# The last two of four token blocks: norm weights from a spread row, transposition behind the last product, additions of two or four tiles

## The chip, the core and the metric

The kernel runs on one core of a Trainium2 chip. A core has TensorE (PE, matrix products and transpositions; PEld is its loading of the stationary operand), VectorE (DVE), ScalarE (ACT), GpSimd (POOL) and SyncE (SP, which here only issues transfers), each with its own queue of instructions that it takes in order. They share an on-chip memory (SBUF) and the products' accumulators (PSUM). Sixteen transfer engines move data between the chip's DRAM and SBUF. The metric is device time in microseconds, the median of three runs.

## The reference

Two layers work on 512 tokens of width 1024, in float32. The change touches only the very end of the second layer, its feed-forward part:

```python
f = rmsnorm(h, ln_ffn_pre[layer])
f = (jax.nn.silu(f @ w_ffn_gate[layer]) * (f @ w_ffn_up[layer])) @ w_ffn_down[layer]
h = h + rmsnorm(f, ln_ffn_post[layer])

def rmsnorm(x, g):
    y = xf * lax.rsqrt(jnp.mean(xf * xf, axis=-1, keepdims=True) + RMS_EPS)
    return (y * g.astype(jnp.float32)).astype(x.dtype)
```

For every token the last product's row of 1024 numbers is scaled by one number of that token (r) and by the 1024 weights `ln_ffn_post`, and added to h, which is the result.

## The kernel before

**Layout.** h lies transposed: a tile of 128 partitions for 128 of the 1024 features, with the 512 tokens along the free axis, and eight such tiles (k = 0 to 7, `h[:, k, :]`). The weights of all norms lie in the tile `gains`, a column of 128 for each k; so `residual` (L841) can take a weight as a scalar per partition.

**The last product.** `feed_forward(1, ...)` works through the 22 blocks of the hidden width in groups (2 to 8, 8 to 14, 14 to 18, 18 to 22; blocks 0 and 1 come first). For each group it makes the hidden values (`sevens`, with the w_gate and w_up loads), and then their product with w_down. These products have the tokens as rows: four token blocks `tb` of 128, each with two halves `dh` of 512 features, `ys[tb][dh]`. Each product of float32 numbers is three products of parts (L193 to L195). The loads of all weights go through four buffers named `raw` of 512 KB each on SyncE's queue, where each waits until VectorE has read what stood in its buffer.

**The tail.** The product of the last group is made block by block in `tail` (L790). For each block and half, 12 products of 512 columns run on TensorE, VectorE adds them to `ys` (L808), ScalarE squares and sums (L811); VectorE adds the sums to v (L813), GpSimd raises v to the power -1/2 to r (L262), and ScalarE scales both halves by r (L832). The second half of the last block is made in two pieces of 256 columns in one PSUM tile, so that TensorE waits with the second for VectorE's addition of the first; there, scaling is shared by VectorE (L827) and ScalarE (L828).

**The end.** `give(tb, order)` (L1347) turns the scaled block by eight transpositions on TensorE (`turned`, L839, into PSUM tiles `yt` with the tag "tr", of which there are two), adds each 128x128 tile to h with its weight (`residual`, L844, one VectorE instruction per tile), and issues the transfer of each group of tiles to `out`. Block tb - 1 is given behind the product of block tb, the last one behind eight products of zeros (`idle`, L88) that occupy TensorE while r is made. The last block's four transfers alternate between SyncE's queue and ScalarE's.

The order within an engine comes from a scheduler that may move an instruction ahead of others written before it, where it depends on nothing among them; the places where that shows are given with the change.

```python
zero = zeros()
for tb in range(TB):
    end = tail(tb)
    if tb:
        give(tb - 1, (range(4), range(4, 8)))
idle(8, zero, end)
give(TB - 1, (range(4, 6), range(2), range(6, 8), range(2, 4)), (nc.sync, nc.scalar))
```

Of the kernel before, what the change touches and what calls it, by code (L numbers as in the profile page):

```python
# [15 lines left out]
P = 128  # L16
T = 512
D = 1024
# [22 lines left out]
def hybrid(ctx: ExitStack, tc: tile.TileContext, i: dict, out: bass.AP):  # L41
# [4 lines left out]
    tp = ctx.enter_context(tc.tile_pool(name="temps", bufs=4))  # L46
    wp = ctx.enter_context(tc.tile_pool(name="weights", bufs=4))
    sp = ctx.enter_context(tc.tile_pool(name="small", bufs=8))
    pp = ctx.enter_context(tc.tile_pool(name="psum", bufs=3, space=PSUM))

    n_of = {}
# [2 lines left out]
    def name(s):  # L54
        n_of[s] = n_of.get(s, 0) + 1
        return f"{s}_{n_of[s]}"
# [10 lines left out]
    def temp(s, shape=(P, T), tag="t", bufs=4, dt=F32):  # L67
        return tp.tile(list(shape), dt, tag=tag, name=name(s), bufs=bufs)

    def small(s, n=4, dt=F32):  # L70
        return sp.tile([P, n], dt, tag=f"s{n}", name=name(s))
# [702 lines left out]
        return mix_tail(0, mixed, ys)  # L774


    def tail_of(xs, load, ys, eps=None, last=False):

        ws = {}
        nk = len(xs)

        def urgent(tb):
            return tc.high_priority() if tb == TB - 1 and not last else ExitStack()

        ss, v, r = small("ss", 12), small("v"), small("r")

        def tail(tb, halfway=None):  # L790
            if not ws:
                for dh in range(2):
                    for kp in range(nk // 2):
                        ws[kp, dh] = load(kp, dh, dh == 1)
            c = slice(tb, tb + 1)
            final = last and tb == TB - 1
            two = small("two", 1) if final else None
            at = [(0, 0, 4), (1, 0, 2), (1, 2, 4)] if final else [(0, 0, 4), (1, 0, 4)]
            for n, (dh, m0, m1) in enumerate(at):
                if m0 == 0:  # L800
                    o = ps("lg" if dh else "mm", s="y")
                cols = slice(m0 * P, m1 * P)
                for k in range(nk):
                    w = [part[:, m0:m1, :] for part in ws[k // 2, dh][k % 2]]
                    end = token_products(o[:, cols], xs[k], w, tb, k == 0, k == nk - 1)
                y = ys[tb][dh][:, cols]
                with urgent(tb):
                    V.tensor_add(y, o[:, cols], y)  # L808
                    junk = temp("sq", (P, T), "sq", 3, BF16)
                    one = ss[:, 3 * tb + n : 3 * tb + n + 1]  # L810
                    A.activation(junk[:, cols], y, AF.Square, scale=1.0 / 32, accum_out=one)  # L811
                    if n == len(at) - 1:
                        V.scalar_tensor_tensor(out=v[:, c], in0=one, scalar=run, in1=eps[:, c] if eps is not None else rms_eps,  # L813
                                               op0=ALU.add, op1=ALU.add)
                    elif n:
                        V.tensor_add(two, run, one)
                        run = two
                    else:
                        run = one
                if halfway and n == 0:  # L820
                    halfway()
            with urgent(tb):
                rsqrt(r[:, c], v[:, c], 1)
            if final:
                for m in (0, 2):
                    cols = slice(m * P, (m + 2) * P)
                    V.tensor_scalar_mul(ys[tb][1][:, cols], ys[tb][1][:, cols], r[:, c])  # L827
                    A.activation(ys[tb][0][:, cols], ys[tb][0][:, cols], AF.Copy, scale=r[:, c])  # L828
                return end
            with urgent(tb):  # L830
                for y in ys[tb]:
                    A.activation(y, y, AF.Copy, scale=r[:, c])  # L832

        return tail, ys

    def turned(ys, k, tbs, out):

        for n, tb in enumerate(tbs):
            PE.transpose(out[:, n * P : (n + 1) * P], ys[tb][k // 4][:, k % 4 * P : (k % 4 + 1) * P], ident)  # L839

    def residual(o, k, cols, post):  # L841

# [217 lines left out]
    def feed_forward(layer, phase, xp, meanwhile=None):  # L1060
# [283 lines left out]
    with tc.tile_pool(name="ffn1", bufs=4) as xp:  # L1344
        tail, ys = feed_forward(1, phase, xp)

    def give(tb, order, queues=(nc.sync,)):  # L1347

        c = (tb * P, (tb + 1) * P)
        for n, some in enumerate(order):  # L1350
            tr = ps("tr", s="yt")
            for x, k in enumerate(some):
                turned(ys, k, (tb,), tr[:, x * P : (x + 1) * P])
            for x, k in enumerate(some):
                residual(tr[:, x * P : (x + 1) * P], k, c, G_FFN_POST + 1)
            k0, k1 = some[0], some[-1] + 1
            queues[n % len(queues)].dma_start(out[:, k0:k1, c[0] : c[1]], h[:, k0:k1, c[0] : c[1]])
# [69 lines left out]
```

## Time and profile before

| | |
|---|---|
| median of three runs | 1115.33 us (1115.09 to 1115.86) |
| the profiled execution | 1114.41 us |
| its span, from the first instruction to the last | 1112.7 us |
| TensorE, VectorE, ScalarE, GpSimd busy | 99%, 80%, 59%, 2% of the span |
| mean granted TensorE clock | 0.999 of full speed |
| read from DRAM, written | 104.71 MB, 2.10 MB |

The profile's page gives busy time, a chain of work that ended last and groups of instructions. Views of the trace behind it list instructions in order of time (start, duration, engine, line, operation, tiles, and in brackets the idle time of the engine just before it with what ended it; xN merges N instructions in a row), sum up busy time and transfers over stretches of time, and group instructions by line and shape. Durations of neighbours in one queue overlap a little: the next instruction starts before the last one's duration is over, so the distance of two starts is shorter than a duration.

### The profile page before, as it was taken

The numbers are of one execution on the slowest core, as the hardware profiler recorded it, in microseconds if no ns is written. First come the engines' busy times: TensorE is split into PE (matmuls) and PEld (weight loads), VectorE is DVE, ScalarE is ACT, GpSimd is POOL, SyncE is SP. The second block draws the span as 40 slices with busy tenths as digits, with TensorE's granted clock in tenths as the row PEclk, the third lists the DMA queues.
The fourth block names the chain that finished last, engine by engine and source line by source line (L and its number), as shares of the span: only waits on it lengthen the run. The fifth ranks groups of instructions, "written<-read, shape, count | busy, mean of one in ns | idle before, by whom it ended". The sixth has DMA issues, their size and how long they took to land.

```text
span 1112.7 us, 19537 instructions
## 1 busy us (share of the span) xinstructions
PE 1103.1 (99%) x7409; PEld 1000.2 (90%) x7409; DVE 891.2 (80%) x1721; ACT 660.5 (59%) x1388; POOL 25.4 (2%) x41
## 2 busy tenths in 40 slices
PE   9999999999999999999999999999999999999998
PEld 6998889999899899998988888889999899899996
DVE  7879558998698588797968889858998598588776
ACT  7775468665265254477647667768665266255453
POOL 0000000000000000001000000000000000000000
PEclk9999999999999999999999999999999999999999
DMA  7522231334134233244232654431125234233222
GB/s 268 159 79 74 88 104 58 114 95 153 57 115 136 58 111 114 77 153 151 78 95 71 159 125 130 129 95 57 58 95 161 67 109 132 65 112 116 77 76 76
DMA packets 63557, 118.12 MB, mean 106 GB/s; under 512 B 5164, under 2 KB 39992, under 8 KB 63464
## 3 DMA queue, kind: packets, MB, share of 16 engines
q1 hardware_dynamic: 62584, 116.05, 34.5%
q8 instruction: 58, 0.95, 0.4%
q0 software_dynamic: 192, 0.52, 0.2%
q10 hardware_dynamic: 688, 0.31, 0.1%
q14 instruction: 35, 0.29, 0.1%
HBM read 104.71 MB, written 2.10 MB: 96 GB/s over the span
## 4 chain that ended last, share of the span: by engine, by line
PE 89%; DVE 5%; ACT 3%; issue 1%; DMA 1%; POOL 0%; SPq 0%; POOLq 0%; DVEq 0%; ACTq 0%
PE y L193 9%; PE y L195 9%; PE y L194 9%; PE a L195 5%; PE a L193 5%; PE a L194 5%; PE e L193 3%; PE e L195 3%; PE x L193 3%; PE x L195 3%; PE e L194 3%; PE x L194 3%; PE ps L195 3%; PE ps L193 3%; PE ps L194 3%; PE v L193 2%
## 5 line engine op out<-in xcount | busy, mean ns | idle before, releaser
L241 ACT CAST whi<-raw 128x512 fp32r<-128x512 f32 x460 | 276.1, 620 | 261.3 <-PE y L195 118.6
L241 DVE TENSOR_TENSOR wlo<-raw,whi 128x512 fp32r<-128x512 f32 x460 | 305.8, 685 | 112.4 <-ACT whi L241 110.0
L193 PE MATMUL y<-whi,fhi 128*128 128x512 f32 (+1 forms) x356 | 139.8, 393 | 0.0
L194 PE MATMUL y<-wlo,fhi 128*128 128x512 f32 (+1 forms) x356 | 139.3, 391 | 0.0
L195 PE MATMUL y<-whi,flo 128*128 128x512 f32 (+1 forms) x356 | 139.3, 391 | 0.0
L193 PE MATMUL x<-xshi,whi 128*128 128x256 f32 x320 | 89.7, 280 | 0.0
L195 PE MATMUL x<-xshi,wlo 128*128 128x256 f32 x320 | 89.7, 280 | 0.0
L195 PE MATMUL a<-xshi,wlo 128*128 128x256 f32 x320 | 89.6, 281 | 0.0
L193 PE MATMUL a<-xshi,whi 128*128 128x256 f32 x320 | 89.6, 280 | 0.0
L194 PE MATMUL x<-xslo,whi 128*128 128x256 f32 x320 | 89.6, 280 | 0.0
L194 PE MATMUL a<-xslo,whi 128*128 128x256 f32 x320 | 89.5, 280 | 0.0
L195 PEld LDWEIGHTS y<-whi,flo 128*128 128x128 f32 x356 | 66.9, 188 | 15.6 <-DVE flo L241 0.2
L193 PEld LDWEIGHTS y<-whi,fhi 128*128 128x128 f32 x356 | 66.8, 188 | 15.0 <-DVE y L808 0.2
L194 PEld LDWEIGHTS y<-wlo,fhi 128*128 128x128 f32 x356 | 66.9, 188 | 14.9 <-DVE wlo L241 0.2
L195 PE MATMUL ps<-xshi,wlo 128*128 128x256 f32 (+1 forms) x224 | 66.7, 299 | 1.3 <-DVE wlo L241 1.3
L193 PE MATMUL ps<-xshi,whi 128*128 128x256 f32 (+1 forms) x224 | 67.7, 303 | 0.0
L194 PE MATMUL ps<-xslo,whi 128*128 128x256 f32 (+1 forms) x224 | 66.5, 297 | 0.0
L194 PEld LDWEIGHTS a<-xslo,whi 128*128 128x128 f32 x320 | 60.3, 188 | 0.3
L193 PEld LDWEIGHTS a<-xshi,whi 128*128 128x128 f32 x320 | 60.3, 188 | 0.3
L195 PEld LDWEIGHTS x<-xshi,wlo 128*128 128x128 f32 x320 | 60.3, 189 | 0.0
L193 PEld LDWEIGHTS x<-xshi,whi 128*128 128x128 f32 x320 | 60.3, 188 | 0.0
L194 PEld LDWEIGHTS x<-xslo,whi 128*128 128x128 f32 x320 | 60.3, 188 | 0.0
(291 smaller groups left out, 3086.7 us busy)
## 6 DMA issues: line engine op xcount, KB each, us to landing
raw<-in_w_gate SPq DMA_DIRECT2D x44, 512.0 KB
raw<-in_w_up SPq DMA_DIRECT2D x44, 512.0 KB
raw<-in_w_down SPq DMA_DIRECT2D x44, 512.0 KB
raw<-in_w_out SPq DMA_DIRECT2D x16, 512.0 KB
raw<-in_w_b_q SPq DMA_DIRECT2D x8, 512.0 KB
raw<-in_w_a_v SPq DMA_DIRECT2D x6, 512.0 KB
raw<-in_w_a_u SPq DMA_DIRECT2D x6, 512.0 KB
raw<-in_w_v SPq DMA_DIRECT2D x6, 512.0 KB
```

The source lines that it names most:

```text
L193: PE.matmul(o, w[0], x[0], start=start, stop=False, skip_group_check=more)
L194: PE.matmul(o, w[0], x[1], start=False, stop=False, skip_group_check=more)
L195: return PE.matmul(o, w[1], x[0], start=False, stop=stop, skip_group_check=more)
L241: last_parts[:] = A.copy(hi, src), (eng or V).tensor_sub(lo, src, hi)
```

## The change

The weights of the last norm are written, by a transfer of 1024 elements of 4 bytes, as a row into a DRAM tile (`row_of_gains`, at the start of the third group of layer 1), and later loaded from there into all 128 partitions of a `raw` buffer (`spread_gains`, behind the first tail). For blocks 2 and 3 (`added`) VectorE multiplies `ys` by that row into new tiles `yg`, ahead of r. ScalarE scales `yg`. The last block's second half is multiplied by r and the row in one VectorE instruction. The additions to h then need no weight and take two or four tiles at once (`give_added`). Block 2 is turned behind the last product (`end`), its last four tiles are added behind the last v (`sums`), there are six products of zeros instead of eight, and the PSUM tiles of the last block have the tags "lg" and "mm", of three buffers each.

```diff
+    def row_of_gains(block):
+        gain_row[0] = dp.tile([1, D], F32, name="row")
+        with tc.issue_after(last_load[0].ins), nc.allow_non_contiguous_dma(reason="one row of gains"):
+            nc.sync.dma_start(gain_row[0].rearrange("o (k p) -> (o k) p", k=KT),
+                              i["gains"][:, block * KT : block * KT + KT].rearrange("p k -> k p"))
+
+    def spread_gains():
+        row = gain_row[0]
+        gain_row[0] = wp.tile([P, D], F32, tag="raw", name=name("raw"), bufs=4)
+        nc.sync.dma_start(gain_row[0], row[0, :].partition_broadcast(P))
...
+            added = last and tb >= TB - 2
             final = last and tb == TB - 1
+            if added:
+                gained[tb] = [plain("yg") for _ in range(2)]
...
                     V.tensor_add(y, o[:, cols], y)
+                    if added and not (final and dh):
+                        V.tensor_mul(gained[tb][dh][:, cols], y, gain_row[0][:, 512 * dh + m0 * P : 512 * dh + m1 * P])
...
                     cols = slice(m * P, (m + 2) * P)
-                    V.tensor_scalar_mul(ys[tb][1][:, cols], ys[tb][1][:, cols], r[:, c])
-                    A.activation(ys[tb][0][:, cols], ys[tb][0][:, cols], AF.Copy, scale=r[:, c])
-                return end
+                    y0, y1 = (y[:, cols] for y in gained[tb])
+                    V.scalar_tensor_tensor(out=y1, in0=ys[tb][1][:, cols], scalar=r[:, c],
+                                           in1=gain_row[0][:, 512 + m * P : 512 + (m + 2) * P],
+                                           op0=ALU.mult, op1=ALU.mult)
+                    A.activation(y0, y0, AF.Copy, scale=r[:, c])
+                return end, total
             with urgent(tb):
-                for y in ys[tb]:
+                for y in gained[tb] if added else ys[tb]:
                     A.activation(y, y, AF.Copy, scale=r[:, c])
+            return end, total
...
+            if layer and gi == 2:
+                row_of_gains(G_FFN_POST + 1)
...
+    def give_added(tb, order, tags, queues=(nc.sync,), end=None, held={}):
+        c = (tb * P, (tb + 1) * P)
+        for n, some in enumerate(order):
+            tr = ps(tags[n], (P, len(some), P), s="yt")
+            k0, k1 = some[0], some[-1] + 1
+            with behind([end] if end else ()):
+                for x, k in enumerate(some):
+                    row_turned(gained[tb], k, tr[:, x, :])
+            with behind(held.get(n, ())):
+                V.tensor_add(h[:, k0:k1, c[0] : c[1]], tr, h[:, k0:k1, c[0] : c[1]])
+            queues[n % len(queues)].dma_start(out[:, k0:k1, c[0] : c[1]], h[:, k0:k1, c[0] : c[1]])
...
     for tb in range(TB):
-        end = tail(tb)
-        if tb:
+        end, sums = tail(tb)
+        if tb == 0:
+            spread_gains()
+        elif tb < TB - 1:
             give(tb - 1, (range(4), range(4, 8)))
-    idle(8, zero, end)
-    give(TB - 1, (range(4, 6), range(2), range(6, 8), range(2, 4)), (nc.sync, nc.scalar))
+    give_added(TB - 2, (range(2), range(2, 4), range(4, 8)), ("tr", "tr", "mm"), end=end, held={2: [sums]})
+    idle(6, zero, end)
+    give_added(TB - 1, (range(4, 6), range(2), range(6, 8), range(2, 4)), ("lg", "mm") * 2, (nc.sync, nc.scalar))
```

Three places in the order of the instructions. Line numbers after the change are higher by up to 46, and buffer numbers differ. First VectorE at the end of the program, before; y_9713 is the second half of the last block, yt_13423 and yt_13433 are block 2's turned tiles, the other yt the last block's:

```order
L816 TENSOR_TENSOR two_13368<-ss_13174 128x1
L844 SCALAR_TENSOR_TENSOR h<-yt_13423,gains,h 128x128 x2
L808 TENSOR_TENSOR y_9713<-y_13385,y_9713 128x256
L844 SCALAR_TENSOR_TENSOR h<-yt_13433,gains,h 128x128 x2
L813 SCALAR_TENSOR_TENSOR v_13175<-ss_13174,two_13368,eps_13170 128x1
L844 SCALAR_TENSOR_TENSOR h<-yt_13433,gains,h 128x128
L827 TENSOR_SCALAR y_9713<-y_9713,r_13176 128x256 x2
L844 SCALAR_TENSOR_TENSOR h<-yt_13433,gains,h 128x128
L844 SCALAR_TENSOR_TENSOR h<-yt_13452,gains,h 128x128 x2
L844 SCALAR_TENSOR_TENSOR h<-yt_13458,gains,h 128x128 x2
L844 SCALAR_TENSOR_TENSOR h<-yt_13464,gains,h 128x128 x2
L844 SCALAR_TENSOR_TENSOR h<-yt_13470,gains,h 128x128 x2
```

The same place after the change; raw_13260 is the spread row, yt_13436, yt_13441 and yt_13446 are block 2's:

```order
L837 TENSOR_TENSOR two_13380<-ss_13178 128x1
L827 TENSOR_TENSOR y_9715<-y_13398,y_9715 128x256
L1387 TENSOR_TENSOR h<-yt_13436,h 128x2x128
L1387 TENSOR_TENSOR h<-yt_13441,h 128x2x128
L834 SCALAR_TENSOR_TENSOR v_13179<-ss_13178,two_13380,eps_13174 128x1
L1387 TENSOR_TENSOR h<-yt_13446,h 128x4x128
L849 SCALAR_TENSOR_TENSOR yg_13379<-y_9715,r_13180,raw_13260 128x256 x2
L1387 TENSOR_TENSOR h<-yt_13465,h 128x2x128
L1387 TENSOR_TENSOR h<-yt_13460,h 128x2x128
L1387 TENSOR_TENSOR h<-yt_13470,h 128x2x128
L1387 TENSOR_TENSOR h<-yt_13475,h 128x2x128
```

All of block 2's additions now stand behind the last addition of y (L808 before, L827 after), two of them ahead of v and one between v and the scaling; none is left behind the scaling. Of the last block's tiles those that ScalarE scales (yt_13465) come first.

TensorE around the second half of the last product, before: four and one transpositions of block 2 stand between the two halves, three behind the last product.

```order
L195 MATMUL y_13385<-whi_13216,flo_12893 128x256
L839 MATMUL yt_13423<-ident,y_9710 128x128 x4
L839 MATMUL yt_13433<-ident,y_9711 128x128
L193 MATMUL y_13385<-whi_13202,fhi_12610 128x256
```

TensorE behind the last product, after: eight transpositions, then the products of zeros, of which the first is shown, then the last block's pairs in another order than they are written in.

```order
L196 MATMUL y_13398<-whi_13220,flo_12897 128x256
L867 MATMUL yt_13436<-ident,yg_13318 128x128 x2
L867 MATMUL yt_13441<-ident,yg_13318 128x128 x2
L867 MATMUL yt_13446<-ident,yg_13319 128x128 x4
L89 LDWEIGHTS zeros_13182
L89 MATMUL idle_13453<-zeros_13182 128x512
```

Nothing of block 2 is left between the halves. On SyncE's queue after the change, the row's transfer stands between the last w_down load of the second group and the w_gate loads of the third:

```order
L170 DMA raw_11828<-in_w_down 128x4x256
L170 DMA raw_11862<-in_w_down 128x4x256
L784 DMA row<-in_gains 1024x1x1
L147 DMA raw_11906<-in_w_gate 128x1024
L147 DMA raw_11908<-in_w_gate 128x1024
```

Before, the w_gate loads followed directly. The spreading load likewise comes right behind the last four w_down loads, ahead of all transfers to `out`.

More of the change, by code (lines that the diff above doesn't have):

```diff
@@ L48, in hybrid @@
     sp = ctx.enter_context(tc.tile_pool(name="small", bufs=8))
+    dp = ctx.enter_context(tc.tile_pool(name="rows", bufs=1, space=bass.MemoryType.DRAM))
     pp = ctx.enter_context(tc.tile_pool(name="psum", bufs=3, space=PSUM))
@@ L774, in layer_a @@
         return mix_tail(0, mixed, ys)
+    gained, gain_row = {}, [None]
+    def row_of_gains(block):
[7 more added lines that the diff above has]
+        nc.sync.dma_start(gain_row[0], row[0, :].partition_broadcast(P))
     def tail_of(xs, load, ys, eps=None, last=False):
@@ L812, in tail @@
                     if n == len(at) - 1:
-                        V.scalar_tensor_tensor(out=v[:, c], in0=one, scalar=run, in1=eps[:, c] if eps is not None else rms_eps,
+                        total = V.scalar_tensor_tensor(out=v[:, c], in0=one, scalar=run, in1=eps[:, c] if eps is not None else rms_eps,
                                                op0=ALU.add, op1=ALU.add)
@@ L838, in turned, with row_turned @@
         for n, tb in enumerate(tbs):
-            PE.transpose(out[:, n * P : (n + 1) * P], ys[tb][k // 4][:, k % 4 * P : (k % 4 + 1) * P], ident)
+            row_turned(ys[tb], k, out[:, n * P : (n + 1) * P])
+    def row_turned(y, k, out):
+        PE.transpose(out, y[k // 4][:, k % 4 * P : (k % 4 + 1) * P], ident)
     def residual(o, k, cols, post):
```

## The prediction

> **What bounds the kernel now.** I read the page first: matrix products fill the whole span, so a change elsewhere only counts where the products have stopped or are made to stop.
>
> ```profile
> PE 1103.1 (99%) x7409; PEld 1000.2 (90%) x7409; DVE 891.2 (80%) x1721; ACT 660.5 (59%) x1388; POOL 25.4 (2%) x41
> ```
>
> The change touches the last 20 us. The timeline of all engines from the last product on (start, duration, what ran) shows the stage that can move:
>
> ```profile
> 1103.76 0.28 PE L195 MATMUL y<-whi,flo 128*128 128x256 f32 x1
> ...
> 1103.88 0.49 PE L839 MATMUL yt<-ident,y 128*128 128x128 f32 x3
> 1104.08 0.42 DVE L808 TENSOR_TENSOR y<-y,y 128x256 f32<-128x256 f32 x1 [0.54 <-PE y L195]
> ...
> 1104.42 0.60 DVE L844 SCALAR_TENSOR_TENSOR h<-yt,gains,h 128x128 f32<-128x128 f32 x2
> ...
> 1104.86 0.19 ACT L811 ACTIVATION_READ_ACCUMULATOR sq<-y 128x1 f32 x1
> 1105.08 0.22 DVE L813 SCALAR_TENSOR_TENSOR v<-ss,two,eps 128x1 f32<-128x1 f32 x1
> ...
> 1105.38 0.55 POOL L262 TENSOR_TENSOR r<-v,mhalf 128x1 f32<-128x1 f32 x1 [6.29 <-DVE v L813]
> 1105.95 0.91 ACT L828 ACTIVATE y<-y,r 128x256 f32<-128x256 f32 x2 [0.91 <-POOL r L262]
> 1105.96 0.61 DVE L827 TENSOR_SCALAR y<-y,r 128x256 f32<-128x256 f32 x2 [0.40 <-POOL r L262]
> 1106.42 0.20 PEld L839 LDWEIGHTS yt<-ident,y 128*128 128x128 f32 x2 [0.83 <-PE idle L88]
> 1106.45 0.93 PE L839 MATMUL yt<-ident,y 128*128 128x128 f32 x4 [0.36 <-DVE y L827]
> 1106.49 2.75 DVE L844 SCALAR_TENSOR_TENSOR h<-yt,gains,h 128x128 f32<-128x128 f32 x9
> ```
>
> The last product ends at 1104.04. Add, square, sum, power and scaling follow one another to 1106.31 (1105.96 + 0.348, half of the x2 row). Then nine residual additions keep VectorE until 1109.24. The first of the nine is left over from block 2; the other eight are block 3's.
>
> After that only transfers run. Windows of the trace (stretch, busy time by engine, granted clock, DMA share, GB/s) show them:
>
> ```profile
> 1104.00:1104.50 0.50, 0.50 (x6) 0.37 (x5) 0.42 (x2) 0.00 (x0) 0.00 (x0) 1.00 0.02 7
> 1104.50:1105.00 0.50, 0.50 (x4) 0.21 (x3) 0.50 (x3) 0.47 (x2) 0.00 (x0) 1.00 0.99 283
> 1108.00:1109.00 1.00, 0.41 (x3) 0.20 (x2) 0.99 (x5) 0.00 (x0) 0.00 (x0) 1.00 1.00 286
> 1109.00:1110.00 1.00, 0.00 (x0) 0.00 (x0) 0.24 (x1) 0.00 (x0) 0.00 (x0) 1.00 0.99 282
> 1110.00:1110.50 0.50, 0.00 (x0) 0.00 (x0) 0.00 (x0) 0.00 (x0) 0.00 (x0) 1.00 0.76 220
> 1110.50:1111.00 0.50, 0.00 (x0) 0.00 (x0) 0.00 (x0) 0.00 (x0) 0.00 (x0) 1.00 0.32 92
> ```
>
> From 1108 to 1110 the transfer engines are full. Data moves until 1110.66 (0.32 of half a microsecond past 1110.5), and 2.0 us of completion follow to the span's end at 1112.7. The queues' table for 1103 to 1112.7 gives the price of a piece:
>
> ```profile
> q1 hardware_dynamic: 1600, 0.79, 28.4%
> q10 hardware_dynamic: 544, 0.26, 9.4%
> ```
>
> Together 37.8% of 9.7 us is 3.67 us for eight pieces of 128 KB: **0.46 us a piece**. From issue to first data I take **0.92 us**: an issue at 1103.57 answers to data at 1104.49 (0.02 of the window that ends at 1104.5).
>
> ```profile
> 1103.57 5.49 SPq L1357 DMA_DIRECT2D out<-h  x4
> ```
>
> **The change part by part.** *The multiplications by the row of weights.* Three 128x512 multiplications join VectorE before the last product, each as long as the 128x512 addition at 1096.76 below: 0.69, and 0.60 from its start to the next (a 128x128 residual takes 0.26 from start to start, by the x5 row). The idle time in front of the additions is their cover:
>
> ```profile
> 1096.76 0.69 DVE L808 TENSOR_TENSOR y<-y,y 128x512 f32<-128x512 f32 x1 [1.87 <-PE y L195]
> 1097.37 0.86 DVE L844 SCALAR_TENSOR_TENSOR h<-yt,gains,h 128x128 f32<-128x128 f32 x3
> ...
> 1098.38 1.38 DVE L844 SCALAR_TENSOR_TENSOR h<-yt,gains,h 128x128 f32<-128x128 f32 x5
> 1100.42 0.69 DVE L808 TENSOR_TENSOR y<-y,y 128x512 f32<-128x512 f32 x1 [0.66 <-PE y L195]
> 1101.86 0.42 DVE L808 TENSOR_TENSOR y<-y,y 128x256 f32<-128x256 f32 x1 [0.74 <-PE y L195]
> ```
>
> They fall one into each gap: 1.87, 0.66 and 0.74, leaving 1.27, 0.06 and 0.14. I cost them at 0. Without cover each would delay the second half of the last product by up to 0.60, since that half waits for the addition at 1101.86.
>
> *The five transpositions taken out from between the halves.* They save nothing: the second half begins when the addition of the first has ended (1101.86 + 0.42 = 1102.28), and it does so with them or without.
>
> ```profile
> 1102.34 0.19 PEld L193 LDWEIGHTS y<-whi,fhi 128*128 128x128 f32 x1 [0.21 <-DVE y L808]
> ```
>
> So the last product still ends at 1104.04. Behind it now stand eight transpositions instead of three (0.11 apart by the x3 row, done by 1104.95) and six idle products instead of eight, which wait for the first two-tile addition and end near 1106.4, before TensorE is wanted at 1106.59.
>
> *Block 2's additions.* ScalarE's operations keep their number and shapes. Before v there were two of 0.26; now there are two 128x256 ones, 0.34 from start to start (1104.08 to 1104.42). v, which ScalarE allows at 1105.05, goes from 1105.08 to 1105.10: **+0.02**. The four-tile addition starts 0.13 behind v and takes 0.60, so VectorE is free at 1105.83, before r at 1105.95. That addition replaces two residuals, one of which stood behind the scaling.
>
> *Block 3's scaling.* The multiplication by r and the row is a scalar_tensor_tensor; the groups by form show 478 ns for such an operation, against 348 now:
>
> ```profile
> L246 DVE SCALAR_TENSOR_TENSOR xslo<-h,gains,xshi 128x256 fp32r<-128x256 f32 x16 | 7.5, 478 | 0.1
> ```
>
> Its first half is ready at 1106.46, ScalarE's first half at 1105.97 + 0.51 = 1106.48, and TensorE now takes ScalarE's tiles first. With the 0.11 from data to weight load (1106.31 to 1106.42) the pair starts at 1106.59 and ends at 1107.03, against 1106.86 now: **+0.17**.
>
> *Block 3's additions.* Eight residuals, held up by two PSUM buffers, become four 128x256 additions of 0.42 (the row at 1104.08): 1107.07 + 3 x 0.34 + 0.42 = 1108.51, against 1109.24. **VectorE gains 0.73.** TensorE delivers all pairs by 1107.65 now that they have buffers of their own.
>
> *The transfers out.* Now block 2's last 256 KB is issued only at 1106.87 (behind the leftover residual, 1106.49 + 0.34), moves from 1107.79 to 1108.71, and pushes block 3's four pieces together; the last, issued at 1109.27 behind the last residual, ends at 1109.27 + 0.92 + 0.46 = 1110.65, which is what the windows show. In the changed kernel block 2's 256 KB leave at 1105.9 and are through at 1107.8. The pieces of block 3 are issued at 1107.5, 1107.85, 1108.2 and 1108.55. Data starts at 1108.44, and four pieces fill the engines for 1.84: **1110.28**. So of 0.73 only **0.38** reach the end; the limit moves from VectorE to the transfer engines. The bounds of this term are 0.73 (pieces don't wait for each other) and 0.
>
> *The row of weights.* Its 1024 elements go over SP's queue right behind the last w_down load of the group and ahead of two w_gate loads, whose landing VectorE does wait for:
>
> ```profile
> 940.63 0.37 SPq L169 DMA_DIRECT2D raw<-in_w_down  x1
> 942.98 0.34 SPq L146 DMA_DIRECT2D raw<-in_w_gate  x1
> ...
> 944.96 0.37 ACT L1015 COPY s<-a 128x256 f32<-128x256 f32 x1
> ...
> 950.03 0.69 DVE L988 TENSOR_TENSOR s<-raw,raw 128x512 f32<-128x512 f32 x1 [0.75 <-DMA raw<-in_w_gate]
> 950.64 0.68 DVE L241 TENSOR_TENSOR flo<-s,fhi 128x512 fp32r<-128x512 f32 x1
> ```
>
> ```profile
> 1092.60 0.23 PE y L193
> ```
>
> Behind that wait stands flo, done at 951.32. It belongs to the third pair of the group; the products begin at about 944.9, when ScalarE copies the last hidden sum, and two pairs of 24 products at 0.23, the step of such products in the chain of waits, put its use at 956. **4.7 us of slack.** No row shows four-byte packets. From the queue row, 544 packets took 9.4% of 16 x 9.7 us, 27 ns each. If a small packet costs at most that, 1024 over 16 engines are 1.7 us and over eight 3.5 us; below lies 0. Even 3.5 is inside the slack: cost 0. [...] The spreading load waits on SyncE for a `raw` buffer; behind it stand only block 0's outputs, at 1093.29, and its first reader comes at about 1094.8. Until then the transfer engines are empty, so it too costs 0:
>
> ```profile
> 1093.29 15.77 SPq L1357 DMA_DIRECT2D out<-h  x8
> ```
>
> ```profile
> 1074.00:1093.00 19.00, 19.00 (x110) 16.31 (x109) 10.98 (x22) 8.86 (x20) 0.55 (x1) 1.00 0.01 2
> ```
>
> **Sum.** Data ends at 1110.28 instead of 1110.66: span 1112.3, the profiled execution 1114.03 instead of 1114.41 (1.7 lie outside the span). That execution lay 0.9 below the median of the runs, 1115.33; carried over, **1114.95 us**.
>
> **The rivals.** *A, the pieces don't queue.* If transfers from the two queues overlap better than my price, the last ends at 1108.55 + 0.92 + 0.46 = 1109.93 and the gain is 0.73: 1114.6. For it speaks that two engines issue; against it, that the share is 1.00 at 286 GB/s with both and 0.99 at 283 with SyncE alone. [...]
>
> *B, the power is slowed.* A VectorE operation beside r can stretch it:
>
> ```profile
> 170.18 0.69 DVE L241 TENSOR_TENSOR xslo<-hs,xshi 128x512 fp32r<-128x512 f32 x1
> 170.34 0.93 POOL L262 TENSOR_TENSOR r<-v,mhalf 128x1 f32<-128x1 f32 x1 [7.51 <-DVE v L813]
> ...
> 1098.54 0.54 POOL L262 TENSOR_TENSOR r<-v,mhalf 128x1 f32<-128x1 f32 x1 [4.91 <-DVE v L813]
> ```
>
> The first ran beside the 128x512 subtraction at 170.18 with both operands in SBUF, the second beside the residuals at 1098.38 with one in PSUM. The new four-tile addition runs beside r and has one in PSUM, so I expect 0.55. If its length decides instead, r comes 0.38 later and eats the gain: 1115.3, no change.
>
> *C, the row jams the loads.* If its 1024 packets ran on one transfer engine, they would take 1024 x 27 ns = 27.6 us; the w_gate loads would land some 21 us late, less 4.7 of slack: 16 us, 1131. With two engines it is 13.8 us and some 2 to 3 past the slack: 1118. From three or four engines on it costs nothing. Against it: pieces of 128 rows fill all engines (1.00 above); for 1024 rows of one element no row tells.
>
> *D, the end doesn't move*, since the last product is late: each multiplication reads what the addition just ahead of it wrote, and if that costs 0.2 more than I take, the gaps with 0.06 and 0.14 left push the last product by 0.3: 1115.3.
>
> **How the numbers follow.** My forecast (1114.95, own range 1114.3 to 1115.6, since the three runs lay within 0.8) gets 0.54, A 0.20, B and D 0.18 together, C 0.05, something else 0.03. From A's low side to B's and D's high side the range is 1113.9 to 1116.1. What can be told from no change is 0.2%, 2.2 us: the stage behind the last product has 8.7 us in all, and A's gain is 0.73, so faster by that gets 0.02 (of the unknown), slower 0.06 (C and the rest of the unknown), within it 0.92.
>
> **What would show it.** Right: nine additions become four ending near 1108.5, data ends near 1110.3 with a share of 1.00 from 1108.5, last product at 1104.0, r at 0.55. Wrong: a later last product (the gaps), a w_gate wait of over 5 us near 950, r at 0.9, or a share below 0.9 in the last two microseconds of data (A).

## The result, and the profile after

| | before | after |
|---|---|---|
| median of 6 runs each, us | 1115.55 (1115.09 to 1115.86) | 1123.30 (1122.47 to 1124.21) |
| ratio after/before | | 1.0066, 95% interval 1.0056 to 1.0076 |
| profiled execution, its span | 1114.41, 1112.7 | 1123.36, 1121.7 |

The kernel became slower by 7.75 us; the prediction had 1114.95 and a range up to 1116.1. Rows of the page of after (busy time; then tenths of a slice of the span, 28 us each):

```profile
PE 1106.0 (99%) x7406; PEld 1002.3 (89%) x7407; DVE 891.8 (80%) x1715; ACT 660.0 (59%) x1388; POOL 24.9 (2%) x41
...
PEclk9999999999999999999999999999999999899999
```

One slice shows a lower TensorE clock; on the page of before all forty read 9. That slice, the 35th, runs from 953 to 981 us, far ahead of the tail that the change is about. The row of weights is transferred just ahead of it. SyncE's own rows there (start, duration of issuing):

```profile
925.01 17.58 SPq L170 DMA_DIRECT2D raw<-in_w_down  x6
942.64 0.76 SPq L784 DMA_DIRECT2D row<-in_gains  x1
944.58 3.17 SPq L147 DMA_DIRECT2D raw<-in_w_gate  x2
```

VectorE's rows (in brackets: idle time before, and what ended it), and then TensorE's:

```profile
961.35 0.69 DVE L1016 TENSOR_TENSOR s<-raw,raw 128x512 f32<-128x512 f32 x1 [10.47 <-DMA raw<-in_w_gate]
961.96 0.68 DVE L242 TENSOR_TENSOR flo<-s,fhi 128x512 fp32r<-128x512 f32 x1
```

```profile
957.27 0.40 PE L195 MATMUL y<-wlo,fhi 128*128 128x512 f32 x1
962.69 0.79 PE L196 MATMUL y<-whi,flo 128*128 128x512 f32 x1 [5.02 <-DVE flo L242]
```

The w_gate wait that was 0.75 is now 10.47, flo comes behind it, and TensorE stands for 5.02 us. Windows of after through that place (stretch; busy time of PE, PEld, DVE, ACT, POOL; granted clock, DMA share, GB/s) show both what jams and what follows. A packet's whole time and size count in the window where it starts, so a share can exceed 1 (1.19 from 950):

```profile
944.00:946.00 2.00, 2.00 (x19) 2.00 (x19) 1.24 (x2) 0.62 (x1) 0.00 (x0) 1.00 0.89 246
946.00:948.00 2.00, 2.00 (x10) 1.64 (x10) 1.32 (x3) 0.89 (x2) 0.00 (x0) 1.00 0.79 11
948.00:950.00 2.00, 2.00 (x10) 1.60 (x9) 1.92 (x4) 1.07 (x3) 0.00 (x0) 1.00 0.10 2
950.00:952.00 2.00, 2.00 (x11) 1.63 (x10) 0.88 (x2) 0.90 (x3) 0.00 (x0) 1.00 1.19 47
952.00:954.00 2.00, 2.00 (x10) 1.65 (x9) 0.00 (x0) 0.32 (x1) 0.00 (x0) 1.00 0.67 23
954.00:956.00 2.00, 2.00 (x10) 1.61 (x10) 0.00 (x0) 0.62 (x1) 0.00 (x0) 1.00 0.59 31
956.00:958.00 2.00, 1.67 (x8) 1.02 (x6) 0.00 (x0) 0.62 (x1) 0.00 (x0) 1.00 0.53 59
958.00:960.00 2.00, 0.00 (x0) 0.00 (x0) 0.00 (x0) 0.00 (x0) 0.00 (x0) 1.00 0.90 311
960.00:962.00 2.00, 0.00 (x0) 0.00 (x0) 0.66 (x2) 0.00 (x0) 0.00 (x0) 0.92 0.17 45
962.00:964.00 2.00, 1.31 (x3) 1.12 (x4) 2.00 (x5) 0.00 (x0) 0.00 (x0) 0.50 0.01 4
...
966.00:968.00 2.00, 2.00 (x7) 1.51 (x6) 0.00 (x0) 0.62 (x1) 0.00 (x0) 0.50 0.87 262
968.00:970.00 2.00, 2.00 (x9) 1.65 (x8) 1.98 (x3) 0.00 (x0) 0.00 (x0) 0.87 0.31 125
```

From 946 to 958 the transfer engines are called busy for over half of the time in all windows but one, yet they move only 2 to 59 GB/s. Windows of before at the same times, in which the w_gate weights move:

```profile
946.00:948.00 2.00, 2.00 (x10) 1.64 (x9) 1.92 (x5) 0.66 (x2) 0.00 (x0) 1.00 0.64 156
948.00:950.00 2.00, 2.00 (x11) 1.63 (x10) 1.28 (x2) 1.00 (x2) 0.00 (x0) 1.00 0.42 166
```

The transfers' table of after, asked for 945 to 947 and then for 947 to 957, says which packets these were:

```profile
DMA packets 1291, 0.27 MB, mean 134 GB/s; under 512 B 1048, under 2 KB 1286, under 8 KB 1291
...
DMA packets 56, 0.23 MB, mean 23 GB/s; under 512 B 0, under 2 KB 0, under 8 KB 56
```

The row's packets have all started by 947. What drags are the packets of w_gate behind them: 56 start in the next 10 us.

At the end of the wait the granted clock falls: 0.92, three windows at 0.50 (that from 964 to 966 too), 0.87. In windows of 0.25 us from 957 to 976 it reads 1.00 or 0.50 in all but the two at the edges, 0.86 from 961.50 and 0.99 from 968.50. Counted as full or half, a window of 2 us with the mean clock c has 4 x (1 - c) us at half speed: 0.32 + 3 x 2.0 + 0.52 = 6.84 us. The chain of waits of after (start, duration, what) shows the price per product, 0.43 instead of 0.23:

```profile
967.75 0.43 PE y L195
...
971.14 0.23 PE y L196
```

From 963.49 to 968.61 there are twelve such steps, each 0.20 too long, 2.4 us in all. The product ahead of them took 0.80 (962.69 to 963.49); in e14 below, at full clock, it is 0.33. Together 2.9. **5.02 + 2.9 = 7.9 us.** That is the whole loss: from the first of the six w_down issues (925.01; before 923.41) to the addition that follows the last product (1113.62; before 1104.08) after takes 188.61 us and before 180.67, **+7.94**.

The tail itself did what the prediction says. Rows of after from that addition on:

```profile
1113.62 0.42 DVE L827 TENSOR_TENSOR y<-y,y 128x256 f32<-128x256 f32 x1 [1.00 <-PE y L196]
...
1114.68 0.22 DVE L834 SCALAR_TENSOR_TENSOR v<-ss,two,eps 128x1 f32<-128x1 f32 x1
1114.81 0.68 DVE L1387 TENSOR_TENSOR h<-yt,h 128x512 f32<-128x512 f32 x1
1114.98 0.54 POOL L263 TENSOR_TENSOR r<-v,mhalf 128x1 f32<-128x1 f32 x1 [6.35 <-DVE v L834]
...
1115.55 0.88 DVE L849 SCALAR_TENSOR_TENSOR yg<-y,r,raw 128x256 f32<-128x256 f32 x2
1116.59 1.42 DVE L1387 TENSOR_TENSOR h<-yt,h 128x256 f32<-128x256 f32 x4 [0.15 <-PE yt L867]
```

and its last windows:

```profile
1119.20:1119.70 0.50, 0.00 (x0) 0.00 (x0) 0.00 (x0) 0.00 (x0) 0.00 (x0) 1.00 0.96 286
1119.70:1120.20 0.50, 0.00 (x0) 0.00 (x0) 0.00 (x0) 0.00 (x0) 0.00 (x0) 1.00 0.24 69
```

Nine additions in 2.75 us (block 3's eight and one left over) have become four in 1.42, and from the addition behind the last product to the span's end it is 8.08 us instead of 8.62. So three terms make the two spans' 9.0: +7.94 at the row, -0.54 in the tail, and +1.60 ahead of 925 us, which e1 below shows not to belong to the change.

### The profile page after: what moved, and what is told of

It reads as the page before. It is cut to its first block, busy times and chain, and to the rows that moved or that the text cites. A ratio compares the mean times of both kernels' runs of the same rounds, so it can differ in the third digit from the quotient of the medians.

```text
span 1121.7 us, 19529 instructions
## 1 busy us (share of the span) xinstructions
PE 1106.0 (99%) x7406; PEld 1002.3 (89%) x7407; DVE 891.8 (80%) x1715; ACT 660.0 (59%) x1388; POOL 24.9 (2%) x41
## 4 chain that ended last, share of the span: by engine, by line
PE 87%; DVE 5%; ACT 3%; DMA 2%; issue 1%; POOL 0%; SPq 0%; POOLq 0%; DVEq 0%; ACTq 0%
PE y L196 9%; PE y L194 9%; PE y L195 9%; PE a L194 5%; PE a L196 5%; PE a L195 5%; PE e L194 3%; PE e L196 3%; PE x L194 3%; PE e L195 3%; PE x L195 3%; PE x L196 3%; PE ps L196 3%; PE ps L194 3%; PE ps L195 3%; PE v L194 2%
```

## The experiments

Theory: the row's small writes hold up the loads behind them, TensorE starves, and its clock falls. The runs stand under three headings. Each was compared with the kernel before on the same chip (its medians: 1115.52 for e1 to e4, 1115.78 for e5 to e8, 1114.88 for e9 to e12, 1115.66 for e13 and e14). The ratios are estimates from all runs of a set and can differ from the quotient of the medians by about 0.001. All measures at one glance; "wait" is VectorE's for w_gate, "stop" TensorE's behind it, "way" the time from the first of the six w_down issues to the addition behind the last product, "tail" from there to the span's end, all of the profiled execution:

| kernel | median us | ratio (95%) | wait | stop | way | tail |
|---|---|---|---|---|---|---|
| before | see above | | 0.75 | 0 | 180.67 | 8.62 |
| after | 1123.30 | 1.0066 (1.0056 to 1.0076) | 10.47 | 5.02 | 188.61 | 8.08 |
| e1_row_only | 1121.60 | 1.0050 (1.0036 to 1.0064) | 9.15 | 3.70 | 187.15 | 8.57 |
| e2_row_late | 1114.66 | 0.9994 (0.9985 to 1.0002) | 0.95 | 0 | 180.66 | 8.00 |
| e3_pieces_32 | 1115.78 | 1.0000 (0.9991 to 1.0009) | 0.94 | 0 | 180.69 | 8.05 |
| e4_row_input | 1114.66 | 0.9991 (0.9983 to 1.0000) | 0.96 | 0 | 180.59 | 8.07 |
| e5_apart | 1116.06 | 1.0004 (0.9994 to 1.0014) | 1.04 | 0 | 180.65 | 8.52 |
| e6_reads | 1115.85 | 1.0001 (0.9991 to 1.0010) | 0.85 | 0 | 180.72 | 8.54 |
| e7_writes | 1119.37 | 1.0026 (1.0017 to 1.0036) | 7.21 | 1.76 | 184.28 | 8.53 |
| e8_half | 1120.01 | 1.0040 (1.0025 to 1.0055) | 8.78 | 3.34 | 185.88 | 8.55 |
| e9_runs | 1119.39 | 1.0038 (1.0025 to 1.0051) | 7.92 | 2.47 | 184.96 | 8.52 |
| e10_by_8 | 1115.27 | 0.9998 (0.9989 to 1.0008) | 4.21 | 0 | 180.65 | 8.50 |
| e11_after | 1122.23 | 1.0054 (1.0039 to 1.0070) | 9.36 | 3.92 | 186.44 | 8.02 |
| e12_warm | 1124.33 | 1.0073 (1.0058 to 1.0088) | 9.79 | 2.04 + 3.5 | 190.55 | 8.00 |
| e13_after | 1121.27 | 1.0050 (1.0036 to 1.0064) | 9.63 | 4.18 | 187.73 | 8.10 |
| e14_warm | 1120.01 | 1.0037 (1.0025 to 1.0050) | 9.43 | 1.68 | 184.91 | 8.04 |

### Is it the row, and only the row?

**e1_row_only**: the kernel before, plus this transfer at the changed kernel's place.

```diff
+            if layer and gi == 2:
+                row_of_gains(G_FFN_POST + 1)
```

> The kernel before, with nothing but the transfer of the row added at the place where the changed kernel has it (nothing reads the row). Theory R (the row's 1024 four-byte elements hold up the w_gate loads behind them, TensorE starves for about 5.0 us and then runs at half clock for about 6.8 us, which costs another 3.4): the whole loss is here without any of the new tail, so 1115.5 + 8.4 = about 1123.9, with a w_gate wait of some 10 us at VectorE and a granted clock of 0.50 behind it. Rival S (the loss comes from the new tail, or from a shift of the whole program): 1115.5, no wait over 1 us there. Rival H (only the starving counts, the clock would have been made up later): about 1120.5.

Rows of e1 on SyncE, VectorE and TensorE:

```profile
925.88 2.31 SPq L170 DMA_DIRECT2D raw<-in_w_down  x2
...
960.90 0.69 DVE L996 TENSOR_TENSOR s<-raw,raw 128x512 f32<-128x512 f32 x1 [9.15 <-DMA raw<-in_w_gate]
...
962.25 0.80 PE L196 MATMUL y<-whi,flo 128*128 128x512 f32 x1 [3.70 <-DVE flo L242]
```

The old tail with the row added loses 6.1 us, somewhat less than expected since the stop is 3.70 here and not 5.02. The loss comes with the row. And up to the row e1's program is that of before, instruction for instruction, yet this execution is at 925.88 where that of before was at 923.41: the early shift varies between executions and isn't the change's.

**e2_row_late**: the changed kernel with the same transfer issued behind the last w_down load.

```diff
-            if layer and gi == 2:
-                row_of_gains(G_FFN_POST + 1)
...
                         ws[kp, dh] = load(kp, dh, dh == 1)
+                if last:
+                    row_of_gains(G_FFN_POST + 1)
```

> The changed kernel with the transfer of the row moved behind the last w_down load, where the transfer engines have nothing to do until the row is spread. Theory R: the row takes its 11 us there beside nothing, so what is left is the gain of the tail alone, 0.4 to 0.7 us: 1114.8 to 1115.1. Rival S (the tail loses): 1123. A rival within R (the row is late and the spread and the first multiplication wait for it): above 1116, with a wait of VectorE for the spread weights near 1093.

Rows of e2 on SyncE, then on VectorE:

```profile
1071.80 0.76 SPq L784 DMA_DIRECT2D row<-in_gains  x1
1084.03 0.35 SPq L791 DMA_DIRECT2D raw<-row  x1
...
1096.34 0.68 DVE L829 TENSOR_TENSOR y<-y,y 128x512 f32<-128x512 f32 x1
1097.05 0.69 DVE L831 TENSOR_TENSOR yg<-y,raw 128x512 f32<-128x512 f32 x1
```

The same 1024 packets now cost nothing (a way of 180.66 against 180.67, no stop), and the first multiplication by the row follows its addition without a wait. Place, not work, made the loss. The transfer itself takes long, though. What SyncE waited for (total, times, longest), and a window of that stretch:

```profile
SPq L791 <- DMA row<-in_gains: 11.4, 1, 11.4
...
1078.00:1080.00 2.00, 2.00 (x20) 2.00 (x19) 0.42 (x1) 0.00 (x0) 0.00 (x0) 1.00 0.00 0
```

SyncE waits 11.4 us for the row to land before it issues the spread. In the window shown, 4 us ahead of the landing, the transfer engines move nothing (share 0.00, 0 GB/s), and the row has not landed. What goes on in that time no row shows.

**e4_row_input**: no such transfer; the host lays out the weights as a row too, and the spread reads that.

```diff
-        nc.sync.dma_start(gain_row[0], row[0, :].partition_broadcast(P))
+        nc.sync.dma_start(gain_row[0], i["g_row"].partition_broadcast(P))
...
+        "g_row": x["ln_ffn_post"][1],
```

> The changed kernel without the row's transfer: the host hands the weights in as a row, and the spread reads that row. Theory R: as with the row moved late, 1114.8 to 1115.1, and the tail's steps as in the changed kernel (VectorE done 0.7 us earlier behind the last product than before, data out 0.4 to 0.7 earlier). Rival S: 1123. Rival L (the 1.6 us by which the changed kernel's profile is late already at 232 us belongs to the change): 1116.5.

1114.66 against 1115.52, 0.86 us less. This and e2 are the versions of the change that don't lose; e4's interval ends at 1.0000, e2's above it, so that either beats the kernel before is likely and not settled. Rival L falls; e1 has a larger early shift without the new tail.

### What about the row holds up the loads?

**e3_pieces_32** moves the same 4 KB at the same place in 128 pieces.

```diff
-            nc.sync.dma_start(gain_row[0].rearrange("o (k p) -> (o k) p", k=KT),
-                              i["gains"][:, block * KT : block * KT + KT].rearrange("p k -> k p"))
+            nc.sync.dma_start(gain_row[0].rearrange("o (p k) -> (o p) k", k=KT),
+                              i["gains"][:, block * KT : block * KT + KT])
```

> The changed kernel with the same 4 KB moved at the same place as 128 pieces of 32 bytes instead of 1024 of four (the weights then stand in another order in the row, so the last two token blocks are multiplied by the wrong weights; work and times are otherwise the same). Theory R, if the count of small pieces sets the time: about an eighth of 11 us, inside the slack of 4.7 us: 1114.8 to 1115.1. Rival D (any DRAM to DRAM transfer in this queue between two loads jams them, whatever its pieces): 1123.

```profile
951.87 0.69 DVE L1016 TENSOR_TENSOR s<-raw,raw 128x512 f32<-128x512 f32 x1 [0.94 <-DMA raw<-in_w_gate]
```

No jam (row of e3's VectorE; a wait of 0.94, no stop): this DRAM to DRAM transfer is harmless. The median lies 0.7 to 1.0 above what was expected, within the interval.

The next four are e1 with another transfer in place of its own. **e5_apart** writes each element 512 bytes from the next; **e6_reads** reads the small elements but writes them to SBUF; **e7_writes** takes them from SBUF; **e8_half** moves half of them.

Their new lines, in that order:

```diff
+        row = dp.tile([D, P], F32, name="row")
+            nc.sync.dma_start(row[:, 0:1].rearrange("(k p) o -> k (p o)", k=KT),
```

```diff
+        row = sp.tile([P, KT, 2], F32, name="row", tag="rowx", bufs=1)
+            nc.sync.dma_start(row[:, :, 0:1],
+                              i["gains"][:, block * KT : block * KT + KT].rearrange("p (k o) -> p k o", o=1))
```

```diff
+            nc.sync.dma_start(row.rearrange("o (k p) -> p k o", k=KT),
+                              gains[:, block * KT : block * KT + KT].rearrange("p (k o) -> p k o", o=1))
```

```diff
+            nc.sync.dma_start(row.rearrange("o (k p) -> (o k) p", k=KT)[0:KT // 2],
+                              i["gains"][:, block * KT : block * KT + KT // 2].rearrange("p k -> k p"))
```

> As the row alone, but each of the 1024 four-byte elements is written 512 bytes from the next in DRAM instead of side by side in 4 KB. Theory W (what holds up the loads is many small writes into the same few lines of DRAM, one after the other): the wait at VectorE for w_gate falls under 2 us and the time to 1115.5. Rival N (1024 four-byte writes cost their 10 us wherever they go) and rival Q (1024 small elements in the queue cost it, reads or writes): the wait stays near 9 to 10 us and the time near 1121.6.

> As the row alone, but the 1024 four-byte elements are read from DRAM and written to SBUF, eight to a partition with a gap between them, so that nothing small is written to DRAM. Theories W and N (small writes to DRAM): no wait over 2 us at w_gate, 1115.5. Rival Q (the count of small elements in the queue), or small reads: a wait near 9 us and 1121.6.

> As the row alone, but its 1024 four-byte elements come out of SBUF, so that DRAM is only written, into the same 4 KB side by side (eight elements of a partition 512 bytes apart, the next partition four bytes on). Theories W, N and Q: wait near 9 to 10 us, about 1121.6. Rival R (small reads from DRAM): 1115.5.

> As the row alone, with half of it: 512 elements of four bytes into 2 KB. If the price goes by elements (some 10 ns each, one after the other), the loads come 5.5 us late instead of 11: the wait at VectorE is about 4 to 5 us, which the slack of 4.7 us just takes up, TensorE waits 0 to 1 us, its clock stays at 1.00, and the time is 1115.5 to 1116.5. If the price is one lump for the transfer: 1121.6.

VectorE's row for w_gate in e5, e6, e7 and e8, in that order:

```profile
952.53 0.69 DVE L996 TENSOR_TENSOR s<-raw,raw 128x512 f32<-128x512 f32 x1 [1.04 <-DMA raw<-in_w_gate]
```

```profile
953.29 0.69 DVE L996 TENSOR_TENSOR s<-raw,raw 128x512 f32<-128x512 f32 x1 [0.85 <-DMA raw<-in_w_gate]
```

```profile
958.36 0.69 DVE L996 TENSOR_TENSOR s<-raw,raw 128x512 f32<-128x512 f32 x1 [7.21 <-DMA raw<-in_w_gate]
```

```profile
958.62 0.69 DVE L996 TENSOR_TENSOR s<-raw,raw 128x512 f32<-128x512 f32 x1 [8.78 <-DMA raw<-in_w_gate]
```

Small reads cost nothing (e6: a wait of 0.85, no stop), small writes into 4 KB of DRAM are enough (e7: 7.21 and 1.76), and the same number of them 512 bytes apart cost nothing (e5: 1.04, no stop). e7's wait is shorter than e1's 9.15, and its ten runs spread from 1116.59 to 1120.84; in three executions of the changed kernel the wait is 10.47, 9.36 and 9.63, so it differs between executions. So it is neither the count of packets nor their size alone: e1 and e5 have 6196 packets under 512 bytes each, and waits of 9.15 and 1.04. What differs is where the writes go. e8 was the surprise: half the elements jam nearly as long (8.78 against 9.15). Neither of its two expectations holds. A price per element would have given 4 to 5; a price for the transfer as a whole is what e5 and e6 speak against.

The author's guess from these waits, put to the test next: a small write waits for the one before it in the same block of DRAM, while blocks proceed side by side. Then the count per block would matter, which e8 leaves as it was. **e9_runs** and **e10_by_8** ask how large a block would be: runs of 16 elements 512 bytes apart, and all elements 8 bytes apart.

```diff
+        row = dp.tile([D // 16, P], F32, name="row")
+        src = i["gains"][:, block * KT : block * KT + KT].rearrange("(g j) k -> k g j", j=16)
+            nc.sync.dma_start(row[:, :16].rearrange("(k g) j -> k g j", k=KT), src)
```

```diff
+        row = dp.tile([D, 2], F32, name="row")
+            nc.sync.dma_start(row[:, 0:1].rearrange("(k p) o -> k (p o)", k=KT),
```

> As the row alone, but the 1024 four-byte elements go into DRAM as 64 runs of 16 elements side by side (64 bytes), 512 bytes from run to run. Theory W64 (writes into the same 64 bytes wait for one another; 16 of them make the 10 us): the wait at VectorE for w_gate stays at 8 to 10 us, TensorE waits 3 to 5 us, about 1120 to 1121.6. Theory W512 (the unit is 512 bytes or more, or the 4 KB as a whole): 16 writes to a unit instead of 128, so about 1.3 us of jam, a wait under 3 us and 1115.5.

> As the row alone, but the elements stand 8 bytes apart in DRAM (8 KB), so that any block of DRAM gets half as many small writes as before, and twice as many blocks are hit. Theories W64 and W512 (the writes to one block go one after the other, blocks go beside each other): the jam halves to about 5 us, VectorE waits 3 to 5 us, TensorE 0 to 1 us, clock 1.00, 1115.5 to 1116.5. Rival T (the total of writes into neighbouring DRAM sets the price): 1120 to 1121.6.

VectorE's row of e9, then that of e10:

```profile
958.11 0.69 DVE L996 TENSOR_TENSOR s<-raw,raw 128x512 f32<-128x512 f32 x1 [7.92 <-DMA raw<-in_w_gate]
```

```profile
954.73 0.69 DVE L996 TENSOR_TENSOR s<-raw,raw 128x512 f32<-128x512 f32 x1 [4.21 <-DMA raw<-in_w_gate]
```

64-byte runs far apart jam almost as the dense row does (7.92 against 9.15); half the density, over twice the stretch, about halves it (4.21). Each wait is from one execution, but the runs agree: all seven of e9 lose (1118.08 to 1122.40), and e10's ten do not (1114.30 to 1116.39). So W512, which forecast a wait under 3 for e9, falls. On the guess a block of 128 bytes falls too: it would get 16 writes in e9 and in e10 alike, but the waits are 7.92 and 4.21. Counted in stretches of 64 bytes, the length of e9's runs, 16 writes go with waits of 7.21 to 10.47, eight with one of 4.21, and two (e3's 32-byte pieces) or one with next to none (0.94 and 1.04, where runs without small writes to DRAM have 0.75 to 0.96). On the guess, some 0.6 to 0.7 us for each of the 16 is an estimate from the 10 us of dragging packets in after and the 11.4 us of e2. What is measured is that the wait goes with how densely the small writes stand. That writes wait for one another, and in blocks of what size, no trace shows: it stays the author's guess.

### How much of the loss is the clock?

**e11_after** and **e13_after** are the changed kernel again, for comparison on the same chip. **e12_warm** puts idle products ahead of the third pair's.

```diff
+                    if layer and gi == 1 and dh == 0 and kp == 2:
+                        o = ps("tr", s="idle")
+                        for _ in range(40):
+                            PE.matmul(o[:, :P], ident_b, ident_b, start=True, stop=True)
```

> The changed kernel again, as it is, so that the next one is compared with it on the same chip: about 1123.

> The changed kernel with 40 idle 128x128 products in front of the third pair's products, where TensorE has to wait for the late w_gate loads. The row and its jam stay. Theory (of the loss some 5 us are the wait itself and 3.4 us come from the granted clock, which falls to 0.50 for 6.8 us because TensorE stood idle): the idle products take 2.5 to 4.5 us of the wait, what is left of it is too short for the clock to fall, so the clock stays at 1.00 and the time falls by 3 to 3.5 us against the changed kernel, to about 1119.8. Rival H (the clock's fall costs nothing, since the weights or VectorE's parts come no faster anyway): as the changed kernel, 1123, or more.

e12 is inconclusive. The first wait went as expected (2.04, clock 1.00 behind it), but the scheduler, with the new products in its plan, put an addition of w_up's weights ahead of four others on VectorE; it waited 4.47 us there, TensorE stood 3.5 us a second time, and the clock fell after all (0.71 from 970 to 972). **e14_warm** has the same idle products and holds that addition where it was in after.

```diff
-                with behind(ended if opens else ()):
+                with behind(ended if opens else pin if pin else ()):
                     u.sums()
+                if not opens:
+                    pin.clear()
...
-                    V.tensor_add(ys[tb][dh], outs[tb], ys[tb][dh])
+                    added = V.tensor_add(ys[tb][dh], outs[tb], ys[tb][dh])
+                if layer and gi == 1 and dh == 0:
+                    pin.append(added)
```

> The changed kernel as it is, beside the next one on the same chip: about 1122 to 1123, TensorE waiting 4 to 5 us near 960 and its granted clock at 0.50 for 3.4 or 6.8 us behind that.

> The changed kernel with 40 idle 128x128 products (2.4 us) in front of the third pair's products, and VectorE's order held to the changed kernel's, so that nothing else moves. Theory C (the fall of the clock costs half of its length, 1.7 to 3.4 us): TensorE's own wait is 1.5 to 2.5 us, the clock stays at 1.00, no second wait follows, and the time is 1.7 to 3.4 us under the changed kernel's, about 1119 to 1120.5. Rival H (at half clock nothing is lost, because the parts of the late weights come no faster than TensorE uses them): the time stays within 0.7 us of the changed kernel's.

Windows of e13, then TensorE's rows and windows of e14:

```profile
960.00:962.00 2.00, 0.00 (x0) 0.00 (x0) 0.93 (x2) 0.00 (x0) 0.00 (x0) 0.82 0.05 20
962.00:964.00 2.00, 1.58 (x4) 1.29 (x5) 2.00 (x4) 0.00 (x0) 0.00 (x0) 0.50 0.01 4
```

```profile
957.38 2.41 PE L1174 MATMUL idle<-ident_b 128*128 128x128 bf16 x40
...
961.99 0.50 PE L196 MATMUL y<-whi,flo 128*128 128x512 f32 x1 [1.68 <-DVE flo L242]
```

```profile
960.00:962.00 2.00, 0.32 (x3) 0.01 (x1) 1.36 (x3) 0.00 (x0) 0.00 (x0) 1.00 0.01 4
962.00:964.00 2.00, 2.00 (x9) 1.66 (x10) 2.00 (x4) 0.00 (x0) 0.00 (x0) 1.00 0.01 4
```

The weights come no earlier in e14 (wait 9.43 against 9.63), but the clock stays, and the way to the last product is 184.91 instead of 187.73, **2.8 us** less in the profiled executions. Its excess over before, 4.24, is mostly 2.41 of idle products and 1.68 of stop. By the medians the gain is 1.26 (1121.27 against 1120.01), between theory C's 1.7 and rival H's 0.7: the changed kernel's executions differ among themselves, and in that of e11 the excess is 186.44 - 180.67 = 5.77 with a stop of 3.92, so only some 1.8 to 1.9 went to the clock. The same subtraction gives 2.8 in e1 and 1.8 to 1.9 in e7, e8 and e9. So theory C holds in the profiled executions, with 1.8 to 2.9 us, while the medians alone would not settle its size.

## Why the prediction was wrong, step by step

**The step that failed** is the row's: "If a small packet costs at most that, 1024 over 16 engines are 1.7 us and over eight 3.5 us", hence "cost 0". As a statement on the packets it was right: all of them started between 945 and 947. The error was to take the time a packet spends on a transfer engine for all that it costs. Behind the last of them the w_gate packets dragged for 10 us, and in e2 SyncE waited 11.4 us for the row to land, with no packet in the transfer engines from 1078 to 1080. In place of 0 the row cost 7.9 us: a w_gate wait of 10.47 (the prediction's own sign of being wrong was over 5), 5.02 of it past the slack, and the clock. The rows of before held no small write to DRAM, the 27 ns came from another kind of packet (0.26 MB in 544, about 480 bytes each), and an unknown bounded by one remote row isn't bounded from above.

Rival C had the right place and the right victim, with a chance of 0.05, but took the number of engines for what decides. In these runs the wait goes with how densely the writes stand in DRAM: 9.15 with elements 4 bytes apart, 7.92 with runs of 16 such elements, 4.21 at 8 bytes, 1.04 at 512.

**The slack of 4.7 us was right.** VectorE's wait less its 0.75 of before, less TensorE's stop, is 10.47 - 0.75 - 5.02 = 4.70 in after, 9.15 - 0.75 - 3.70 = 4.70 in e1, 7.92 - 0.75 - 2.47 = 4.70 in e9. A wait of up to 5.45 costs nothing, and so e10's 4.21 did not.

**A term was missing**: what happens when TensorE stops. Rival C priced only the stop. The clock's fall added 1.8 to 2.9 us in the profiled executions, 2.9 of 7.94 in after, and 1.3 by the medians of e13 and e14.

**The tail was right.** From the addition behind the last product: v at +1.06 (forecast 1105.10 - 1104.08 = +1.02), the four-tile addition done by 1115.49 just before r allows the scaling at 1115.55, r 0.54 as forecast against rival B's 0.93, the first two-tile addition at +2.97 (+2.99), the last ending at +4.39 (+4.43), the data at +6.2 (+6.20; 0.24 of the last window). Rival A, no queueing, would have ended the data 0.35 earlier; the share of 0.96 at 286 GB/s in the window ahead speaks against it. Over the table, the old tail takes 8.50 to 8.62, mean 8.54 of eight, and the new one 8.00 to 8.10, mean 8.05 of eight: a gain of 0.50, forecast 0.38. The data's end came as forecast; the rest of the gain lies behind it, where from the last data to the span's end it is 1.9 us in after and 2.0 in before.

**The multiplications, the transpositions and the prediction's rival D**: without a jam the way is 180.59 to 180.69 with the new tail (e2, e3, e4) and 180.65 to 180.72 with the old (before, e5, e6, e10). So the three multiplications and the moved transpositions cost nothing, as forecast, and D falls. The spread cost nothing either (e2).

Where the row does cost 0, as the forecast took it, the rest of the sum fits: it forecast 0.38 less than before, and e2 and e4 are 0.86 less (1114.66 against 1115.52) with intervals that hold 0.38. They do not fix the size of the gain; the tail's 0.50 does that better.

## What to carry to other kernels

Here a transfer that writes 1024 elements of 4 bytes side by side into DRAM held up the load behind it far longer than its own packets took: they had all started within 2 us, and the wait for the load was 7.2 to 10.5 us instead of 0.75. What helped was to write longer pieces (0.94), to hand the data in laid out (0.96), or to issue the transfer where nothing needed soon follows (no stop). A wait that makes TensorE stop should be priced with the clock that it loses, here 1.8 to 2.9 us behind stops of 1.8 to 5.0 us, while stops of 1.68 and 2.04 left it at 1.00. And a cost that no row of the profile shows is not bounded by the nearest row when that row is of another kind of access.

## What the hardware showed that was not expected

The writes' own packets look cheap while the price appears elsewhere: in after 1048 packets under 512 bytes start between 945 and 947 beside the tail of other loads, then 56 packets of w_gate take 10 us. In e2 the transfer engines show no packet from 1078 to 1080, and the row has still not landed; that comes only at about 1084.0.

The clock at half speed lasts 3.4 or 6.8 us in seven executions, counted from windows of 2 us as above: 6.84 in after, e1 and e13, 3.40 to 3.44 in e7, e8, e9 and e11. In e7 by these windows 0.92 + 2.0 + 0.52 = 3.44:

```profile
960.00:962.00 2.00, 2.00 (x8) 1.58 (x8) 2.00 (x4) 0.00 (x0) 0.00 (x0) 0.77 0.20 18
962.00:964.00 2.00, 2.00 (x6) 1.51 (x6) 0.17 (x2) 0.62 (x1) 0.00 (x0) 0.50 0.75 272
964.00:966.00 2.00, 2.00 (x9) 1.61 (x8) 1.93 (x4) 0.00 (x0) 0.00 (x0) 0.87 0.67 238
```

Which of the two it is does not go by the stop alone: e1's of 3.70 brought 6.84, e11's of 3.92 brought 3.40. Nor was a long stop needed: e7's was 1.76 us, and TensorE was at work again, at 959.71, when its clock fell near 961.1. Stops of 1.68 (e14) and 2.04 (e12) left the clock alone. What tells these apart stays open. Of e7's ten runs five have a mean granted clock of 0.999 or 1.000 (1116.59 to 1119.35 us) and five one of 0.997 or 0.998 (1119.38 to 1120.84), which suggests that the clock does not fall in every run of one kernel.
